# Low parts of the weights last in a block, partly on POOL, and a third output block at the last head of a matrix-memory layer

## The chip, the cores and the metric

The kernel runs on one core of a Trainium2 chip. The metric is the device time of one execution in microseconds (us): the median of three runs. One further execution was recorded by the hardware profiler. PE, ACT, DVE, POOL and SP are the tensor, scalar, vector, general (GpSimd) and sync engines; SP issues the loads of weights.

## The reference

A decoder trunk of two layers, each a token mixer and a gated MLP with a short convolution, with an RMSNorm before each. It has 320 tokens: one prompt of 256 and eight sequences of eight sampled tokens. The model width is 1024. Layer a mixes by spatial gating. Layer b, where the change lies, is a matrix memory (mLSTM) with 8 heads, keys of 128 and values of 256. Cut to what matters, for a head and its running state `C`, `n`, `m`:

```python
p = x @ w_in                       # q/k before the convolution, v, o, and the gates i and f
qk = silu(causal_dwconv(qk_pre, ...))
ig = i_pre + b_i;  lf = log_sigmoid(f_pre + b_f)
b = cumsum(lf);  D = b[t] - b[s] + ig[s]  (s <= t)
m_t = max(b + m, max_s D);  sc = (q @ k.T) * exp(D - m_t);  w = exp(b + m - m_t)
num = w * (q @ C) + sc @ v;  den = w * (q @ n) + sum(sc)
h = num / max(|den|, exp(-m_t))
C_new = decay * C + (k * g).T @ v
y = (sigmoid(o) * groupnorm(h)) @ w_out
```

The kernel takes all tokens of the prompt as one chunk. The outputs include the new states of the prompt and of the eight samples.

## The kernel before

**Products with weights.** A weight block is 1024 x 128 (8 k-tiles of 128 x 128), used against all 320 tokens. So that the product is nearly exact in a reduced input type, a block `raw` is split in two: the high part `wh`, a cast on ACT (L127), and the low part `wl` = raw - wh, a subtraction on DVE (L130). The tokens are split likewise into `xh` and `xl`. `chunk()` issues three matmuls per k-tile (wh with xh, wh with xl, wl with xh), 24 for a block of 8. `weights()` writes out the queue `wq` of all blocks in order; `prefetch()` loads up to four blocks ahead from SP (four buffers `raw`) and splits one block ahead (three buffers each of `wh` and `wl`); `take()` hands out the next one.

**What sets the order.** PE runs in the order in which the program issues its matmuls. On ACT, DVE, POOL and SP a scheduler orders the instructions; each engine then works through its own queue in order, and waits on semaphores of the others. Products of blocks go to three PSUM banks (`pm`), all else in layer b to five others.

**The gates.** `gates()` computes the rows of the input and forget gates for 8 heads, while PE multiplies the first six blocks of `b_win` (head 0: two of q/k, two of v, two of o). The rows pass through a multiply by the norm's row `rb`, a bias, a log-sigmoid in two tables on ACT (Exp, Ln), and two scans on DVE: the running sum `b` (L593) and the running maximum `M` (L598). From these come `X` (L609 and L610: M and the weights of the old state, split in high and low part), which the matmul `pMb` spreads over the partitions, and the rows `RS`, which are transposed to columns (`pt`, `cols`). In the trace most of these rows are called `g`.

**A head.** `scores(h)` makes the decay weights `w` from pMb (ACT), masks them with selects on POOL (L684 to L689) and multiplies the scores with them (`Pf`, split into `Ph`, `Pl`). `state_split` splits the old state `C` into `Ch` (ACT) and `Cl` (DVE, L758); `inter(h, i)` multiplies it with the queries `Qz`; `numer(h)` adds the products within the chunk to `num` and issues the statistics of the group norm, down to the power `sl` on POOL (L805). `k_nat` and `v_nat` transpose k and v (`pk`, `pv`), make `kgh`, `kgl`, `kgs` and, on POOL, `kgz` (L737); `v_nat` makes `vh`, `vl`. `state_prompt` (`pCp`) and `state_sample` (`pcs`) make the new states. `o_epi` makes the output gate (`o_b` on DVE, `th_o` on ACT). `finish(h)` transposes the normed head (`phn`) and makes its output halves `yhb` (ACT, L861) and `ylb` (DVE, L862). The loop over heads puts the work of head h-1 between the blocks of head h.

**The output product.** `b_wo` has eight output blocks over 16 k-tiles, two per head. Their first halves (k-tiles 0 to 7) are placed between heads 4 and 6 (`EARLY_OUT`). At the last head, `begin(0)` and `begin(1)` start the second halves of blocks 0 and 1 with the six k-tiles that are ready (8 to 13); the end of the layer closes them with the two of the last head and does the other six.

Of the kernel before, what the change touches and what calls it, by code (L numbers as in the profile page):

```python
# [19 lines left out]
NB, NS = 8, 8  # L20
# [17 lines left out]
class Net:  # L38
# [19 lines left out]
    def weights(self):  # L58

        I = self.I  # L60
        q = []

        def add(w, b, *groups, k0=0):
            for kn in groups:
                q.append((w, b, k0, kn))
                k0 += kn

        for b in range(4):
            add(I["a_wv"], b, 4, 4)
# [12 lines left out]

        ffn(0)
        add(I["b_wg"], 0, 8)
        for h in range(NH):
            for r in range(6):
                if (h, r) == (NH - 1, 4):
                    for b in (0, 1):
                        add(I["b_wo"], b, 6, k0=8)
# [3 lines left out]
        for b in range(KD):  # L93
            if b < 2:
                add(I["b_wo"], b, 2, k0=14)
            else:
                add(I["b_wo"], b, 8, k0=8)
        ffn(1)
        self.wq = q
        self.loaded, self.halved, self.used = [], [], 0  # L100

    AHEAD, SPLIT_AHEAD = 4, 1
    EARLY_OUT = {(4, 5): (0, 1), (5, 3): (2,), (5, 5): (3, 4), (6, 3): (5,), (6, 5): (6, 7)}

    def prefetch(self, n, m):

        nc = self.nc
        while len(self.loaded) < min(n, len(self.wq)):
            w, b, k0, kn = self.wq[len(self.loaded)]
            raw = self.wraw.tile([P, 8, P], F32, tag="raw", name="raw")  # L110
            nc.sync.dma_start(raw[:, :kn, :], w[b, :, k0:k0 + kn, :])
            self.loaded.append(raw)
        while len(self.halved) < min(m, len(self.wq)):
            i = len(self.halved)
            raw, kn = self.loaded[i], self.wq[i][3]
            self.loaded[i] = None
            wh = self.wsp.tile([P, 8, P], F32R, tag="wh", name="wh")
            wl = self.wsp.tile([P, 8, P], F32R, tag="wl", name="wl")
            if self.wq[i][0] is self.I["b_wg"]:

                nc.scalar.copy(wh[:, :, 64:], raw[:, :, 64:])
                nc.scalar.copy(wl[:, :, :64], raw[:, :, :64])
                nc.vector.tensor_tensor(wl[:, :, 64:], raw[:, :, 64:], wh[:, :, 64:].bitcast(F32), op=SUB)
                self.halved.append((None, wl))
                continue
            if i:
                self.last_split = nc.scalar.copy(wh[:, :kn, :], raw[:, :kn, :])  # L127
            else:
                nc.vector.tensor_copy(wh[:, :kn, :], raw[:, :kn, :])
            nc.vector.tensor_tensor(wl[:, :kn, :], raw[:, :kn, :], wh[:, :kn, :].bitcast(F32), op=SUB)  # L130
            self.halved.append((wh, wl))

    def take(self):
# [386 lines left out]
    def layer_b(self):  # L520
# [5 lines left out]
        with ExitStack() as ctx:  # L526
# [23 lines left out]
            def gates(rp):  # L550
                bif = rp.tile([8, 2 + NB], F32, name="bif")
                rst = rp.tile([8, 2, T], F32, name="rst")
                selr = rp.tile([40, NH, P], F32, name="selr")
# [9 lines left out]
                nc.gpsimd.memset(sel.bitcast(F32), 0.0)  # L563
                m0 = bif[:, 2:2 + NB]
# [27 lines left out]
                nc.vector.scalar_tensor_tensor(z, z, 0.0, az, op0=ALU.min, op1=SUB)  # L592
                nc.vector.tensor_tensor_scan(b, rst[:, 0, :], z, 0.0, op0=MULT, op1=ADD)  # L593
# [4 lines left out]
                nc.vector.tensor_tensor_scan(M, rst[:, 1, :], aM, -1e30, op0=ADD, op1=MAX)  # L598
                nc.vector.tensor_tensor(m, b, M, op=ADD)
# [4 lines left out]
                ML = M[:, TP + NS - 1::NS]  # L604
                nc.vector.tensor_copy(Xf[:, 0:T], M)
                nc.vector.tensor_tensor(seg(wi[:, :64]), m0.unsqueeze(2).to_broadcast([8, NB, NS]), seg(M[:, TP:]), op=SUB)
# [7 lines left out]

                nc.vector.tensor_copy(RS[0:8, 0:T], a)
                nc.vector.tensor_scalar(g[:, :TP], a[:, :TP], M[:, TP - 1:TP], None, op0=SUB)
# [157 lines left out]
            def numer(h):  # L774
                s = S[h]
                Ph, Pl, dec = s["P"]
                mv, dn = mvs[h % 2], dns[h % 2]
                num = [self.psa.tile([P, 512], F32, tag="pa", name="num") for _ in range(2)] + [s["num2"]]
# [6 lines left out]
                mm3(d, Ph[:, P:TP], Pl[:, P:TP], vh[:, 0, :], vl[:, 0, :], True, False)  # L785
                mm3(d, Ph[:, TP:384], Pl[:, TP:384], vh[:, 1, :], vl[:, 1, :], False, True)
                ns = hp.tile([64, CW], F32, tag="ns", name="ns", bufs=1)
                nc.scalar.copy(ns, num[2][64:, :CW])
# [106 lines left out]

            part = {}

            def begin(m):

                part[m] = self.psm.tile([P, 512], F32, tag="pm", name="pm")  # L900
                self.chunk(part[m], lambda k: Y[8 + k], True, False)

            for h in range(NH):
                if h:
# [9 lines left out]
                    early(h, 1)  # L914
                    v_epi(h, 0, blk())
                    state_prompt(h - 1)
# [22 lines left out]
                if h and not last:  # L939
                    state_sample(h - 1, 3)  # L940
                k_nat(h)
                v_nat(h)
                if h:
                    inter(h, 0)
                for i in (2, 3):
                    state_split(h, i)
                early(h, 5)
# [3 lines left out]
            begin(1)  # L951
            inter(h, 1)
            for i in (2, 3):
                inter(h, i)
            numer(h)
            o_epi(h, 0, blk())
            state_prompt(h)
            o_epi(h, 1, blk())
            finish(h)
            for i in range(4):  # L960
                state_sample(h, i)
            nc.sync.dma_start(O["nP"], nP)
            nc.sync.dma_start(O["nS"], nS)
            for m in range(KD):
# [3 lines left out]
                else:  # L968
                    self.chunk(ps, lambda k: Y[14 + k], False, True)
                self.residual_norm(m, ps, V_FFN + 8)  # L970


    def run(self):
        nc, tc, I, O = self.nc, self.tc, self.I, self.O
        with tc.tile_pool(name="const", bufs=1) as cp, tc.tile_pool(name="xp", bufs=1) as xp, \
# [21 lines left out]
            self.layer_a()  # L997
            self.ffn(0, V_MIX + 8)
            self.layer_b()
            self.ffn(1, None)  # L1000

# [13 lines left out]
def _lay_out(i):  # L1015
# [29 lines left out]
    for c in (0, 64):  # L1045
# [3 lines left out]
    a["b_wo"] = _blocks(i["b_w_out"][0])  # L1049
    a["b_if"] = np.ascontiguousarray(np.concatenate(  # L1050
        [i["b_bias_i"].T, i["b_bias_f"].T, i["state_mlstm_m"][0].T], axis=1))
    a["b_state"] = np.ascontiguousarray(i["state_mlstm_conv"][0].reshape(24, 16, P).transpose(2, 1, 0))
# [13 lines left out]
    a["bdt"] = ((q[:, None] // NS == q[None, :] // NS) & (q[:, None] <= q[None, :])).astype(f)  # L1066
    seg = np.zeros((8, 2, T), f)
    starts = [0] + list(range(TP, T, NS))
# [37 lines left out]
```

## Time and profile before

| | |
|---|---|
| median of three runs | 977.37 us (975.83 to 977.41) |
| profiled execution, its time | 975.58 us |
| its span | 973.9 us |
| its mean granted clock of PE | 0.996 |
| busy: PE, DVE, ACT, POOL | 961.7, 697.6, 514.5, 103.2 us |
| matmuls | 6513 |
| instructions | 17241 |
| layer b in the trace | about 425 to 731 us |

Engines work side by side, so their busy times do not add up. A line of a group names a source line, the engine, the operation, the output and inputs with shapes, a count, and after the bar the busy time, the mean of one in ns, and the idle time just before with what ended it. A line of the timeline begins with the start and the duration in us, and ends, where the engine waited, with the wait and what released it. Instructions of one kind that follow each other closely are one line there, with their count behind an x.

### The profile page before, as it was taken

To read this page: it belongs to the slowest core of one execution; us is meant where nothing else is said; L and a number is where in the kernel's file an instruction comes from. 1 tells how busy PE (TensorE), PEld (TensorE's weight loads), DVE (VectorE), ACT (ScalarE), POOL (GpSimd) and SP (SyncE) were. 2 spreads that over 40 slices of the span, in tenths; PEclk is the share of its full clock that TensorE was granted. 3 is DMA by queue.
4 is the path that set the end of the run, shared out by engine and by line. 5 is a ranking of instruction groups with operands and counts; after the bars stand their busy time and mean duration, and the time that the engine had idled before them with its cause. 6 is when DMAs were issued, how large, how long until landed. Compare 5 with 4: busy or idle time off the path is not lost.

```text
span 973.9 us, 17241 instructions
## 1 busy us (share of the span) xinstructions
PE 961.7 (99%) x6513; PEld 944.8 (97%) x6513; DVE 697.6 (72%) x1348; ACT 514.5 (53%) x922; POOL 103.2 (11%) x286
## 2 busy tenths in 40 slices
PE   9999999999999999999999999999999999999996
PEld 7889999999999999999999999999999999999996
DVE  6658975577777755469999978887787777775442
ACT  6557543454454443348766756565565455544432
POOL 3200000010000000013231111111101000000000
PEclk9999999999999999999999999999999999999998
DMA  8745444444444455555565565553464444445541
GB/s 264 234 136 165 128 129 151 151 148 152 150 144 147 146 153 152 154 176 174 175 205 168 185 200 167 170 189 120 140 204 138 152 150 152 151 147 149 152 125 54
DMA packets 56308, 154.60 MB, mean 159 GB/s; under 512 B 6642, under 2 KB 18290, under 8 KB 56226
## 3 DMA queue, kind: packets, MB, share of 16 engines
q1 hardware_dynamic: 56226, 153.51, 49.6%
q8 instruction: 51, 0.84, 0.4%
q14 instruction: 31, 0.25, 0.1%
HBM read 141.55 MB, written 11.94 MB: 158 GB/s over the span
## 4 chain that ended last, share of the span: by engine, by line
PE 82%; issue 10%; DVE 5%; ACT 2%; DMA 0%; POOL 0%; SPq 0%; DVEq 0%; POOLq 0%; ACTq 0%
PE pm L47 69%; PE pv_a L47 6%; PE num L47 2%; PE pcs L47 1%; PE pmix L47 1%; DVE wl L130 1%; DVE bcv L648 1%; DVE Cl L758 1%; PE pv L50 0%; ACT wh L127 0%; PE psc L47 0%; PE pCp L47 0%; PE phn L50 0%; DMA xT<-in_xT 0%; PE pg L47 0%
## 5 line engine op out<-in xcount | busy, mean ns | idle before, releaser
L127 ACT CAST wh<-raw 128x1024 fp32r<-128x1024 f32 (+2 forms) x253 | 257.0, 1016 | 341.4 <-PE pm L47 164.1
L130 DVE TENSOR_TENSOR wl<-raw,wh 128x1024 fp32r<-128x1024 f32 (+2 forms) x254 | 299.9, 1181 | 131.8 <-ACT wh L127 128.8
L47 PE MATMUL pm<-xh,wh 128*128 128x320 f32 x1216 | 378.1, 311 | 0.0
L47 PE MATMUL pm<-xh,wl 128*128 128x320 f32 x1216 | 376.0, 309 | 1.1 <-DVE wl L130 1.1
L47 PE MATMUL pm<-xl,wh 128*128 128x320 f32 x1216 | 375.6, 309 | 0.0
L47 PEld LDWEIGHTS pm<-xh,wl 128*128 128x128 f32 x1216 | 228.3, 188 | 1.6 <-DVE wl L130 1.6
L47 PEld LDWEIGHTS pm<-xh,wh 128*128 128x128 f32 x1216 | 228.4, 188 | 0.3
L47 PEld LDWEIGHTS pm<-xl,wh 128*128 128x128 f32 x1216 | 228.4, 188 | 0.3
L47 PE MATMUL pm<-yh_f,wh 128*128 128x320 f32 x352 | 109.0, 310 | 0.0
L47 PE MATMUL pm<-yh_f,wl 128*128 128x320 f32 x352 | 108.5, 308 | 0.0
L47 PE MATMUL pm<-yl_f,wh 128*128 128x320 f32 x352 | 108.5, 308 | 0.0
L47 PEld LDWEIGHTS pm<-yl_f,wh 128*128 128x128 f32 x352 | 66.1, 188 | 0.0
L47 PEld LDWEIGHTS pm<-yh_f,wh 128*128 128x128 f32 x352 | 66.1, 188 | 0.0
L47 PEld LDWEIGHTS pm<-yh_f,wl 128*128 128x128 f32 x352 | 66.1, 188 | 0.0
L442 DVE SCALAR_TENSOR_TENSOR fcv<-fpad,vecs,fcv 128x336 f32<-128x336 f32 x88 | 49.6, 565 | 2.2 <-ACT fcv L440 0.7
L239 DVE TENSOR_TENSOR xT<-pm,xT 128x320 f32<-128x320 f32 x40 | 19.5, 490 | 41.9 <-PE pm L47 41.9
L47 PE MATMUL pm<-ylb,wh 128*128 128x320 f32 x128 | 39.9, 312 | 0.5 <-DVE ylb L862 0.4
L47 PE MATMUL pm<-yhb,wh 128*128 128x320 f32 x128 | 40.0, 312 | 0.4 <-ACT yhb L861 0.4
L47 PE MATMUL pm<-yhb,wl 128*128 128x320 f32 x128 | 39.6, 309 | 0.0
L47 PE MATMUL pm<-yh_a,wh 128*128 128x320 f32 x128 | 39.6, 309 | 0.0
L47 PE MATMUL pm<-yh_a,wl 128*128 128x320 f32 x128 | 39.5, 308 | 0.0
L47 PE MATMUL pm<-yl_a,wh 128*128 128x320 f32 x128 | 39.5, 308 | 0.0
(269 smaller groups left out, 1386.5 us busy)
## 6 DMA issues: line engine op xcount, KB each, us to landing
raw<-in_f_up SPq DMA_DIRECT2D x88, 512.0 KB, 3.3
raw<-in_b_win SPq DMA_DIRECT2D x48, 512.0 KB, 3.7
raw<-in_f_dn SPq DMA_DIRECT2D x32, 448.0 KB, 3.3
C<-in_C SPq DMA_DIRECT2D x32, 258.0 KB, 3.4
raw<-in_a_win SPq DMA_DIRECT2D x16, 512.0 KB, 3.3
raw<-in_a_wo SPq DMA_DIRECT2D x16, 512.0 KB, 3.8
raw<-in_f_dn SPq DMA_DIRECT2D x16, 512.0 KB, 3.5
out_Cs<-C SPq DMA_DIRECT2D x32, 256.0 KB, 2.9
```

The costliest lines, as they stand in the source:

```text
L47: self.pin(self.nc.tensor.matmul(out, lhsT, rhs, start=start, stop=stop))
L127: self.last_split = nc.scalar.copy(wh[:, :kn, :], raw[:, :kn, :])
L130: nc.vector.tensor_tensor(wl[:, :kn, :], raw[:, :kn, :], wh[:, :kn, :].bitcast(F32), op=SUB)
L239: self.nc.vector.tensor_tensor(x, ps[:, :T], x, op=ADD)
L442: nc.vector.scalar_tensor_tensor(cv, pd[:, i:i + NC], self.vec(w + i * KF), cv, op0=MULT, op1=ADD)
L648: nc.vector.scalar_tensor_tensor(cv, pd[:, i:i + NC], self.vec(w + 16 * i), cv, op0=MULT, op1=ADD)
L758: nc.vector.tensor_tensor(Cl, C0, Ch.bitcast(F32), op=SUB)
```

## The change

It has five parts.

1. In layer b alone (`low_last`), `chunk()` issues the 16 products of a block that use `wh` first, then the 8 that use `wl`.
2. For 18 of the 48 blocks of `b_win` (blocks 2 to 5, and the two v blocks of heads 1 to 7, among them 8 and 9) the low part is computed on POOL instead of DVE.
3. The two gates lie in one tile of 40 partitions (input gate in 0 to 7, forget gate in 32 to 39), so that one multiply and one add serve both; two rows are written in place, so two copies go. The bias and the scan's constants are laid out to match by the host.
4. `numer()` is cut in two: the statistics (`stats`) are issued behind the next block of PE, and the scheduler has to place them behind the last split of weights on ACT and on the engine of the last low part.
5. The order at the first and last heads: at head 0 two `state_split` come before `k_nat`; at the last head `begin(0)` takes four k-tiles instead of six, `inter(7, 0)` and one `state_split` come behind `begin(1)`, and a third block, `begin(2)`, is issued behind the last `pcs`. The queue of weights follows.

```diff
+    POOL_LOW = (2, 3, 4, 5) + tuple(6 * h + r for h in range(1, NH) for r in (2, 3))
+    low_last = False
...
-            nc.vector.tensor_tensor(wl[:, :kn, :], raw[:, :kn, :], wh[:, :kn, :].bitcast(F32), op=SUB)
+            w, b, _, _ = self.wq[i]
+            eng = nc.gpsimd if w is self.I["b_win"] and b in self.POOL_LOW else nc.vector
+            self.last_low = eng.tensor_tensor(wl[:, :kn, :], raw[:, :kn, :], wh[:, :kn, :].bitcast(F32), op=SUB)
...
+    def behind_split(self):
+        with self.tc.issue_after(self.last_split.ins), self.tc.issue_after(self.last_low.ins):
+            yield
...
     def chunk(self, ps, rhs, first, last):
         (wh, wl), kn = self.take()
-        for k in range(kn):
-            xh, xl = rhs(k)
-            self.mm(ps[:, :T], wh[:, k, :], xh, first and k == 0, False)
-            self.mm(ps[:, :T], wh[:, k, :], xl, False, False)
-            self.mm(ps[:, :T], wl[:, k, :], xh, False, last and k == kn - 1)
+        for sweep in ((0, 1) if self.low_last else (2,)):
+            for k in range(kn):
+                xh, xl = rhs(k)
+                if sweep != 1:
+                    self.mm(ps[:, :T], wh[:, k, :], xh, first and k == 0, False)
+                    self.mm(ps[:, :T], wh[:, k, :], xl, False, False)
+                if sweep:
+                    self.mm(ps[:, :T], wl[:, k, :], xh, False, last and k == kn - 1)
...
-                ig, z, az, b, a, M, m, aM, g = [row("g" + str(i)) for i in range(9)]
+                b, m, aM, g = [row("g" + str(i)) for i in range(4)]
+                zi, az = [rp.tile([40, T], F32, name=n) for n in ("zi", "az")]
+                ig, z, az = zi[:8], zi[32:], az[32:]
+                a, M = RS[0:8, 0:T], Xf[:, 0:T]
...
-                nc.vector.tensor_tensor(z, gr[32:40], self.rb[32:40, :], op=MULT)
-                nc.vector.tensor_tensor(ig, gr[0:8], self.rb[0:8, :], op=MULT)
+                nc.vector.tensor_tensor(zi, gr[:40], self.rb[:40, :], op=MULT)
                 qk_epi(0, 0, p0)
-                nc.vector.tensor_scalar(z, z, bif[:, 1:2], None, op0=ADD)
-                nc.vector.tensor_scalar(ig, ig, bif[:, 0:1], None, op0=ADD)
+                nc.vector.tensor_scalar(zi, zi, bif[:, 0:1], None, op0=ADD)
...
-                nc.vector.tensor_copy(Xf[:, 0:T], M)
...
-                nc.vector.tensor_copy(RS[0:8, 0:T], a)
...
-                    v_epi(h, 0, blk())
+                    ps = blk()
+                    with self.behind_split():
+                        stats(h - 1)
+                    v_epi(h, 0, ps)
...
             begin(1)
-            inter(h, 1)
-            for i in (2, 3):
+            inter(h, 0)
+            state_split(h, 3)
+            for i in (1, 2, 3):
                 inter(h, i)
             numer(h)
-            o_epi(h, 0, blk())
+            ps = blk()
+            stats(h)
+            o_epi(h, 0, ps)
             state_prompt(h)
             o_epi(h, 1, blk())
             finish(h)
             for i in range(4):
                 state_sample(h, i)
+            begin(2)
...
-                    self.chunk(ps, lambda k: Y[14 + k], False, True)
+                    self.chunk(ps, lambda k: Y[done[m] + k], False, True)
```

More of the change, by code (lines that the diff above doesn't have):

```diff
@@ L1 @@
-from contextlib import ExitStack
+from contextlib import ExitStack, contextmanager
 import numpy as np
@@ L87, in weights @@
                 if (h, r) == (NH - 1, 4):
-                    for b in (0, 1):
-                        add(I["b_wo"], b, 6, k0=8)
+                    add(I["b_wo"], 0, 4, k0=8)
+                    add(I["b_wo"], 1, 6, k0=8)
                 add(I["b_win"], 6 * h + r, 8)
@@ L92, in weights @@
                     add(I["b_wo"], b, 8)
[L93 to L97, printed above, removed]
+        add(I["b_wo"], 2, 6, k0=8)
+        add(I["b_wo"], 0, 4, k0=12)
+        for b in (1, 2):
+            add(I["b_wo"], b, 2, k0=14)
+        for b in range(3, KD):
+            add(I["b_wo"], b, 8, k0=8)
         ffn(1)
@@ L550, in gates @@
             def gates(rp):
-                bif = rp.tile([8, 2 + NB], F32, name="bif")
-                rst = rp.tile([8, 2, T], F32, name="rst")
+                bif = rp.tile([40, 1 + NB], F32, name="bif")
+                rst = rp.tile([40, 2, T], F32, name="rst")
                 selr = rp.tile([40, NH, P], F32, name="selr")
@@ L563, in gates @@
                 nc.gpsimd.memset(sel.bitcast(F32), 0.0)
-                m0 = bif[:, 2:2 + NB]
+                m0 = bif[:8, 1:1 + NB]
                 def row(name, n=T):
                     return rp.tile([8, n], F32, name=name)
-                ig, z, az, b, a, M, m, aM, g = [row("g" + str(i)) for i in range(9)]
+                b, m, aM, g = [row("g" + str(i)) for i in range(4)]
+                zi, az = [rp.tile([40, T], F32, name=n) for n in ("zi", "az")]
+                ig, z, az = zi[:8], zi[32:], az[32:]
                 Xf = row("Xf", 392)
+                a, M = RS[0:8, 0:T], Xf[:, 0:T]
                 wi = row("wi", 72)
@@ L592, in gates @@
                 nc.vector.scalar_tensor_tensor(z, z, 0.0, az, op0=ALU.min, op1=SUB)
-                nc.vector.tensor_tensor_scan(b, rst[:, 0, :], z, 0.0, op0=MULT, op1=ADD)
+                nc.vector.tensor_tensor_scan(b, rst[32:, 0, :], z, 0.0, op0=MULT, op1=ADD)
                 nc.vector.tensor_tensor(a, ig, b, op=SUB)
@@ L597, in gates @@
                 nc.vector.tensor_tensor(aM[:, TP::NS], a[:, TP::NS], m0, op=MAX)
-                nc.vector.tensor_tensor_scan(M, rst[:, 1, :], aM, -1e30, op0=ADD, op1=MAX)
+                nc.vector.tensor_tensor_scan(M, rst[:8, 1, :], aM, -1e30, op0=ADD, op1=MAX)
                 nc.vector.tensor_tensor(m, b, M, op=ADD)
@@ L786, in numer, with stats @@
                 mm3(d, Ph[:, TP:384], Pl[:, TP:384], vh[:, 1, :], vl[:, 1, :], False, True)
+                s["num"] = num
+            def stats(h):
+                s = S[h]
+                num, mv, dn = s.pop("num"), mvs[h % 2], dns[h % 2]
                 ns = hp.tile([64, CW], F32, tag="ns", name="ns", bufs=1)
@@ L894, in blk @@
                 return self.block(KD, self.x_rhs)
-            part = {}
+            part, done = {}, {}
             def begin(m):
                 part[m] = self.psm.tile([P, 512], F32, tag="pm", name="pm")
+                n = self.wq[self.used][3]
                 self.chunk(part[m], lambda k: Y[8 + k], True, False)
+                done[m] = 8 + n
             for h in range(NH):
@@ L940, in layer_b @@
                     state_sample(h - 1, 3)
+                if not h:
+                    for i in (2, 3):
+                        state_split(h, i)
                 k_nat(h)
@@ L943, in layer_b @@
                 if h:
-                    inter(h, 0)
-                for i in (2, 3):
-                    state_split(h, i)
+                    if not last:
+                        inter(h, 0)
+                    for i in (2,) if last else (2, 3):
+                        state_split(h, i)
                 early(h, 5)
@@ L951, in layer_b @@
             begin(1)
-            inter(h, 1)
-            for i in (2, 3):
+            inter(h, 0)
+            state_split(h, 3)
+            for i in (1, 2, 3):
                 inter(h, i)
             numer(h)
-            o_epi(h, 0, blk())
+            ps = blk()
+            stats(h)
+            o_epi(h, 0, ps)
             state_prompt(h)
@@ L998, in run @@
             self.ffn(0, V_MIX + 8)
+            self.low_last = True
             self.layer_b()
+            self.low_last = False
             self.ffn(1, None)
@@ L1049, in _lay_out @@
     a["b_wo"] = _blocks(i["b_w_out"][0])
-    a["b_if"] = np.ascontiguousarray(np.concatenate(
-        [i["b_bias_i"].T, i["b_bias_f"].T, i["state_mlstm_m"][0].T], axis=1))
+    a["b_if"] = np.zeros((40, 1 + NB), w.dtype)
+    a["b_if"][:8] = np.concatenate([i["b_bias_i"].T, i["state_mlstm_m"][0].T], axis=1)
+    a["b_if"][32:, 0] = i["b_bias_f"][0]
     a["b_state"] = np.ascontiguousarray(i["state_mlstm_conv"][0].reshape(24, 16, P).transpose(2, 1, 0))
@@ L1066, in _lay_out @@
     a["bdt"] = ((q[:, None] // NS == q[None, :] // NS) & (q[:, None] <= q[None, :])).astype(f)
-    seg = np.zeros((8, 2, T), f)
+    seg = np.zeros((40, 2, T), f)
     starts = [0] + list(range(TP, T, NS))
```

2 lines of the change are left out of this document (1 added, 1 removed).

## The prediction

> **What bounds the kernel now.** I read the page first (engine shares, costliest groups), then the windows of layer b, the waits of PE, and the timeline around each wait.
>
> ```profile
> span 973.9 us, 17241 instructions
> PE 961.7 (99%) x6513; PEld 944.8 (97%) x6513; DVE 697.6 (72%) x1348; ACT 514.5 (53%) x922; POOL 103.2 (11%) x286
> L130 DVE TENSOR_TENSOR wl<-raw,wh 128x1024 fp32r<-128x1024 f32 (+2 forms) x254 | 299.9, 1181 | 131.8 <-ACT wh L127 128.8
> ```
> ```profile
> 436.00:470.00 34.00, 32.75 (x231) 31.89 (x229) 32.59 (x82) 30.05 (x62) 11.64 (x30) 1.00 0.46 155
> 540.00:665.00 125.00, 125.00 (x901) 124.98 (x900) 102.58 (x239) 73.99 (x161) 19.06 (x36) 1.00 0.55 176
> ```
> ```profile
> PE pm L47 <- DVE wl L130: 1.1, 2, 0.7
> PE pm L47 <- ACT yhb L861: 0.4, 1, 0.4
> PE pm L47 <- DVE ylb L862: 0.4, 2, 0.2
> PE num L47 <- DVE Cl L758: 0.3, 2, 0.2
> ```
>
> The columns of the windows are the stretch, its length, and the busy time of PE, weight load, DVE, ACT and POOL. PE works in 961.7 of 973.9 us, and the change leaves the number of matmuls as it is. In the middle of layer b (540 to 665 us) PE is busy in all 125 us, so nothing that relieves DVE there can shorten anything. Only two places of layer b have time to give: the stage of the gates and head 0 (436 to 470 us: PE 32.75 of 34, while DVE has 32.59 and is the busiest engine but for PE), and the last head. The waits name the four things that PE is short of: low parts of weights, the last head's output halves and the low parts of the matrix memory. Their size comes from the starts of the matmuls:
>
> ```profile
> 453.38 0.31 PE L47 MATMUL pm<-xl,wh 128*128 128x320 f32 x1
> 456.60 0.31 PE L47 MATMUL pm<-xh,wl 128*128 128x320 f32 x1
> 446.90 0.31 PE L47 MATMUL pm<-xl,wh 128*128 128x320 f32 x1
> 447.88 0.31 PE L47 MATMUL pm<-xh,wh 128*128 128x320 f32 x1
> 469.05 0.30 PE L47 MATMUL pm<-xl,wh 128*128 128x320 f32 x1
> 470.29 0.31 PE L47 MATMUL pm<-xh,wh 128*128 128x320 f32 x1
> 703.88 0.31 PE L47 MATMUL pm<-yhb,wh 128*128 128x320 f32 x1
> 706.14 0.31 PE L47 MATMUL pm<-yhb,wl 128*128 128x320 f32 x1
> ```
>
> From the first pair, 22 matmuls start in 3.22 us, 0.147 us each. From 446.90 to 447.88 two starts take 0.98 us instead of 0.29 (0.69 lost, a wait for wl); from 469.05 to 470.29 two take 1.24 (0.95 lost, wl again); from 703.88 to 706.14 five take 2.26 instead of 0.73 (1.53 lost, on the last head's halves). The two waits for Cl and the other one for ylb are 0.5 us together by the view and, with the restart that made 0.64 of the last head's waits into 1.53, some 1.2. So about 4.4 us is all that the change can win. A measurement of this kernel can tell about 0.2%, 1.95 us, from no change.
>
> **Low parts last.** In a block of 8 k-tiles the 16 products with wh now come first, so wl is wanted 16 x 0.147 = 2.35 us after the block's start instead of 0.29, and the wh buffer comes free 8 x 0.147 = 1.17 us earlier. Both known waits for wl are under 1 us, so this alone removes them: 0.69 at the gates, 0.95 behind head 0. In the heads between, PE has no wait and it is worth 0.
>
> **Eighteen low parts on POOL.** A wl costs DVE 1.18 us. POOL's price is not in the trace for this operation; the nearest rows are these, and they also show what the two engines do to each other:
>
> ```profile
> L737 POOL TENSOR_TENSOR kgz<-kgs,mk 128x1024 fp32r<-128x1024 f32 x8 | 15.2, 1898 | 65.5 <-DVE kgs L736 65.5
> L296 POOL TENSOR_TENSOR ws_a<-ws_a,trit 128x1024 f32<-128x1024 f32 x1 | 2.4, 2411 | 0.0
> ```
> ```profile
> 456.47 1.29 DVE L758 TENSOR_TENSOR Cl<-C,Ch 128x516 fp32r<-128x516 f32 x2
> 458.23 1.90 POOL L737 TENSOR_TENSOR kgz<-kgs,mk 128x1024 fp32r<-128x1024 f32 x1 [3.20 <-DVE kgs L736]
> 459.23 2.06 DVE L758 TENSOR_TENSOR Cl<-C,Ch 128x516 fp32r<-128x516 f32 x2
> 678.04 0.85 POOL L805 TENSOR_TENSOR sl<-t,mhalf 128x3 f32<-128x3 f32 x1 [6.51 <-DVE t L803]
> 501.54 1.76 POOL L805 TENSOR_TENSOR sl<-t,mhalf 128x3 f32<-128x3 f32 x1 [3.14 <-DVE t L803]
> 501.37 1.22 DVE L130 TENSOR_TENSOR wl<-raw,wh 128x1024 fp32r<-128x1024 f32 x1
> ```
>
> I take 1.90 us (eight cases, the same size and output type) and keep 2.41 as the other end. The pair of Cl takes 1.29 us alone, but 2.06 where it meets kgz: kgz ends at 460.13, and 460.13 + 1.29 = 461.42 is nearly the pair's end at 461.29. So DVE stood until POOL was through. The other way round, sl takes 0.85 us alone and 1.76 where a wl of DVE runs from 501.37 to 502.59. I read this as exclusion: an instruction of DVE that reads two operands from SBUF and a tensor operation of POOL do not run beside each other, and whoever is in holds it to its end. An instruction of DVE that reads PSUM leaves POOL room to get in. Then moving a wl does not take 1.18 from DVE: it puts 1.90 in its place wherever DVE's neighbours read SBUF.
>
> [...]
>
> Six of the eighteen (blocks 2 to 5, 8 and 9) lie at the gates and head 0, the other twelve in heads 2 to 7, two each. There DVE is busy in 102.58 of 125 us, 18% of it is free, and a head has at least six blocks of 24 x 0.147 = 3.5 us, so 3.8 us of DVE free; exclusion costs at most 2 x (1.90 - 1.18) = 1.4. I take 0; if that cover were gone, up to 1.4 each. Head 0 has no such cover.
>
> **Gates in one tile.** One multiply and one add of DVE go, and two copies:
>
> ```profile
> 445.42 0.31 DVE L615 COPY RS<-g 8x320 f32<-8x320 f32 x1
> 445.65 0.81 DVE L598 TENSOR_TENSOR_SCAN g<-rst,g 8x320 f32<-8x320 f32 x1
> 446.39 1.19 DVE L130 TENSOR_TENSOR wl<-raw,wh 128x1024 fp32r<-128x1024 f32 x1
> 448.38 0.31 DVE L605 COPY Xf<-g 8x320 f32<-8x320 f32 x1
> 450.22 0.56 DVE L610 TENSOR_TENSOR X<-Xf,X 8x392 fp32r<-8x392 f32 x1
> 450.92 1.22 DVE L130 TENSOR_TENSOR wl<-raw,wh 128x1024 fp32r<-128x1024 f32 x1
> 451.21 0.42 PE L47 MATMUL pMb<-X,sel 128*128 128x392 f32 x1
> ```
>
> The chain to watch ends in X, which pMb needs: X is done at 450.78, PE arrives at 451.21. The first saved multiply and add lie ahead of the logarithm, which ACT's table loads hold, so they bring 0. Behind it the copies go (2 x 0.31) and so does the wl of block 5 (1.19, now on POOL). But in the new order of DVE the wl of block 6 stands ahead of the second scan and that of block 7 ahead of the first copy to X (before, they stood behind X, at 450.92 and after): + 2 x 1.2. Sum 2.4 - 0.62 - 1.19 = +0.6. Block 5's POOL instruction falls among scans, subtractions and bcv, which read SBUF: by exclusion + 1.9, and 0.1 for block 4's. X comes at 450.78 + 2.6 = 453.4, and pMb 2.2 us later than before; without exclusion X comes at 451.4, pMb 0.2 later. (The wait of 0.69 that goes is inside these figures.)
>
> **Head 0 behind it.** POOL's queue is in order, and the new one has the wl of block 8 ahead of the memsets and of head 0's selects:
>
> ```profile
> 449.71 0.47 DVE L845 TENSOR_TENSOR o_b<-pm,rb 128x320 f32<-128x320 f32 x1
> 450.22 0.47 ACT L847 ACTIVATE th_o<-o_b 128x320 f32<-128x320 f32 x1
> 451.06 1.05 ACT L127 CAST wh<-raw 128x1024 fp32r<-128x1024 f32 x1 [0.37 <-PE pm L47]
> 451.57 0.21 POOL L879 MEMSET Ps<- 128x128 f32 x1 [2.83 <-issue]
> 453.90 0.54 POOL L684 TENSOR_SCALAR_AFFINE_SELECT w<-w 128x128 f32<-128x128 f32 x2
> 454.75 0.28 POOL L689 TENSOR_SCALAR_AFFINE_SELECT w<-w 64x64 f32<-64x64 f32 x1
> 457.20 0.39 PE L47 MATMUL num<-Cl,Qz 128*128 128x258 f32 x1 [0.17 <-DVE Cl L758]
> ```
>
> Memsets take 451.57 to 453.90, selects 1.13 more. The wl of block 8 waits for its wh, and that cast stands behind th_o on ACT, which waits for o_b on DVE, queued behind the gate chain. With that chain 2.6 later: o_b at 452.3, th_o 452.8 to 453.3, wh to 454.3, wl to 456.2, memsets to 458.5, selects to 459.6. Then the new DVE order has a short Pf, a vl (0.7 us together) and the first Cl (0.65); Pf and vl read PSUM, so kgz gets in right there and holds Cl for 1.9. Cl ends at 459.6 + 1.9 + 0.65 = 462.15; before, the first of the pair at 456.47 ended at 457.12. So the first num is 5.0 us later, the delay of pMb included. What waits behind: every later matmul, since PE is in program order. Without exclusion, wh is done at 450.7 to 452.1, wl 1.9 later, selects end at 456.0 to 457.4, Cl at 457.4 to 458.8: 0.3 to 1.7 later, mean 1.0.
>
> **The last head.** begin(2), 18 matmuls, and 4 of block 0 now stand between the last pcs and the first product that needs yhb and ylb: 22 x 0.147 = 3.2 us.
>
> ```profile
> 705.29 0.55 DVE L862 SCALAR_TENSOR_TENSOR ylb<-y_b,gnh,yhb 128x320 fp32r<-128x320 f32 x1
> ```
>
> The halves were ready at 705.84, and even with one more wl (1.2) ahead of them that is 707.0, against a need at 703.88 + 3.2 = 707.1. The 1.53 goes. The third PSUM bank is held longer, but bank 0 is closed 2 blocks before it is wanted again: 0. The reordered inter and pv save 0 to 0.5 at the earlier wait for ylb, since the Cl behind it is late next. 1.5 to 2.0, I take 1.8. Splitting numer moves DVE work behind a split and, with no PE wait there, costs 0 (at most one wl, 1.2, if DVE were late).
>
> **Sum**, against the profiled execution (span 973.9, time 975.58, so 1.7 around the span; it lies 1.79 under the median 977.37): +5.0 - 0.95 - 1.8 = +2.25, a profiled time of 977.8, and on the median 979.6.
>
> **Rivals.**
> - A, *no exclusion where it counts*: POOL slips in beside instructions of DVE that read PSUM. For it: some of DVE's work there (o_b, cols, vl, bpad) reads PSUM. Against: the pair of Cl. +1.0 - 0.95 - 1.8 = -1.75: 975.6, from -2.7 to -0.8 by the ends.
> - B, *head 0 costs nothing*, the one that ends faster: wh buffers free 1.17 us earlier put block 8's cast ahead of th_o's wait, and its wl on POOL is over when the selects' operand arrives. Then only the gains stay, -2.75, with 2.0 for the last head -2.95: 974.6 and 974.4. It decides in head 0: whether the first num's Cl ends before 457.12 + 2.75 = 459.9; later than that the change loses. The order on ACT (cast behind th_o) speaks against it.
> - C, *POOL's subtraction takes 2.41*: block 4's holds bcv and the logarithm 1.0 longer, blocks 5 and 8 0.5 each: 2.0, of which 0.5 meets slack: 981.1.
>
> [...]
>
> **How the numbers follow.** Forecast 0.42 (975.58 + 2.25 is just over the bound: slower 0.36, same 0.06), A 0.27 (same 0.18, faster 0.09), B 0.23 (faster 0.22, same 0.01), C 0.08 (slower). Faster 0.31, same 0.25, slower 0.44. The range goes from B's far end (974.4) less 0.8, half of the 1.58 between the runs shown, to C's 981.1 plus 1.4 if block 9's POOL instruction delays head 0 as well: 973.6 to 982.5. The forecast's own range is 978.5 to 981.
>
> **What would show it.** Right: a Cl or scan of DVE stretched beside a wl of POOL; wl on POOL near 1.9; pMb waiting near 453.4 and head 0's selects near 458.5; no wait on wl in layer b; no gap behind the last pcs. Wrong: selects before 456, pMb without a wait, or gaps in heads 1 to 6, where I expect none.

## The result

| | before | after |
|---|---|---|
| median | 977.41 us (975.83 to 977.9, 5 runs) | 986.47 us (985.57 to 987.16, 5 runs) |
| ratio | | 1.0095 (1.008 to 1.0109) |
| profiled execution, its span | 973.9 us | 984.6 us |

The change is 9.1 us slower. I had forecast slower, by 2.2: the direction holds, and the size is outside the range (982.5 at most).

First, where the time lies. The span is 10.7 us longer. These are the first memset of the gates, an addition to the residual late in head 6, and the last one of layer b, each in the timeline of before and then of after:

```profile
425.43 0.42 POOL L561 MEMSET RS<- 128x384 f32 x1
661.89 0.49 DVE L239 TENSOR_TENSOR xT<-pm,xT 128x320 f32<-128x320 f32 x1 [1.32 <-PE pm L47]
728.49 0.49 DVE L239 TENSOR_TENSOR xT<-pm,xT 128x320 f32<-128x320 f32 x1 [0.50 <-PE pm L47]
```
```profile
426.74 0.42 POOL L578 MEMSET RS<- 128x384 f32 x1
671.42 0.49 DVE L255 TENSOR_TENSOR xT<-pm,xT 128x320 f32<-128x320 f32 x1 [1.90 <-PE pm L47]
739.28 0.49 DVE L255 TENSOR_TENSOR xT<-pm,xT 128x320 f32<-128x320 f32 x1 [1.03 <-PE pm L47]
```

Layer b begins 1.31 us later, although nothing ahead of it was changed; among the profiled runs below, this memset lies anywhere from 424.99 to 427.31. So 1.3 of the 10.7 is scatter of layer a and has to be taken off before stages are compared. The gates and the heads to head 6 then lose 9.53 - 1.31 = 8.2 us, the last head 10.79 - 9.53 = 1.3.

The longest waits of PE in layer b in the trace of after, and four windows (the first with PE, weight load, DVE, ACT and POOL as before; the others of PE alone, with its granted clock behind the bracket):

```profile
PE pt L50 <- ACT RS L634: 3.6, 1, 3.6
PE num L47 <- DVE Cl L774: 3.2, 3, 2.2
```
```profile
436.00:470.00 34.00, 27.85 (x169) 26.43 (x168) 29.82 (x57) 23.26 (x45) 18.63 (x29) 0.90 0.48 155
480.00:660.00 180.00, 180.00 (x1305) 1.00 0.55 181
...
457.00:458.00 1.00, 1.00 (x5) 0.50 0.89 348
...
467.00:468.00 1.00, 1.00 (x5) 0.50 0.24 93
```

No wait for wl is left, as forecast. In its place PE stands 3.6 us ahead of pt (the transposed gate rows), then 1.0 and 0.5 at the first num, and 2.2 in the last head. From 480 to 660 us it is busy throughout, with 1305 matmuls as before: the low parts on POOL there cost nothing. And one thing was in no step of the prediction: between 436 and 470 us the granted clock of PE is 0.90 on the mean, because it falls to 0.50 twice; a matmul then starts every 0.27 instead of 0.147 us.

What POOL and DVE do to each other, in the group of the low parts on POOL and in the timeline of after:

```profile
L136 POOL TENSOR_TENSOR wl<-raw,wh 128x1024 fp32r<-128x1024 f32 x18 | 44.6, 2480 | 49.0 <-ACT wh L131 35.7
```
```profile
438.77 2.51 POOL L136 TENSOR_TENSOR wl<-raw,wh 128x1024 fp32r<-128x1024 f32 x1 [1.43 <-ACT wh L131]
439.26 2.40 DVE L664 SCALAR_TENSOR_TENSOR bcv<-bpad,vecs,bcv 128x344 f32<-128x344 f32 x1
441.69 0.49 ACT L666 ACTIVATE bth<-bcv 128x344 f32<-128x344 f32 x1 [1.22 <-DVE bcv L664]
446.42 3.12 POOL L136 TENSOR_TENSOR wl<-raw,wh 128x1024 fp32r<-128x1024 f32 x1 [4.28 <-ACT wh L131]
447.20 2.52 DVE L613 COPY g<-RS 8x320 f32<-8x320 f32 x1
450.27 1.21 DVE L136 TENSOR_TENSOR wl<-raw,wh 128x1024 fp32r<-128x1024 f32 x1
451.41 0.81 DVE L616 TENSOR_TENSOR_SCAN Xf<-rst,g 8x320 f32<-8x320 f32 x1
456.16 0.56 DVE L627 TENSOR_TENSOR X<-Xf,X 8x392 fp32r<-8x392 f32 x1
456.77 0.69 PE L47 MATMUL pMb<-X,sel 128*128 128x392 f32 x1 [0.18 <-DVE X L627]
456.81 2.37 POOL L136 TENSOR_TENSOR wl<-raw,wh 128x1024 fp32r<-128x1024 f32 x1 [3.30 <-ACT wh L131]
461.45 0.54 POOL L700 TENSOR_SCALAR_AFFINE_SELECT w<-w 128x128 f32<-128x128 f32 x2
462.50 2.03 DVE L713 TENSOR_TENSOR Qz<-qw,Qz 128x64 fp32r<-128x64 f32 x1
462.56 1.89 POOL L753 TENSOR_TENSOR kgz<-kgs,mk 128x1024 fp32r<-128x1024 f32 x1
464.84 0.36 PE L47 MATMUL num<-Ch,Qz 128*128 128x258 f32 x1 [1.01 <-DMA C<-in_C]
465.71 0.39 PE L47 MATMUL num<-Cl,Qz 128*128 128x258 f32 x1 [0.51 <-DVE Cl L774]
```

This is the forecast's chain, later at each step. Beside block 4 (at 438.77) bcv takes 2.40 us (0.58 elsewhere), and ACT stands 1.22 us for it, ahead of the table load of the logarithm (1.28 us, at 442.20). Beside block 5 (446.42) a plain copy of 8x320, a form that took 0.31 before, takes 2.52, until POOL ends at 449.54. Block 6's wl goes ahead of the second scan. X is done at 456.72, block 8's wl (456.81) holds back the selects, and kgz comes in beside the small Qz (0.21 before, 2.03 here). For the first num the view names a load of C; but the C that it needs had been cast at 461.41, while Qz, which it reads too, was ready only at 464.53.

### The profile page after: what moved, and what is told of

It reads as the page before. It is cut to its first block, busy times and chain, and to the rows that moved or that the text cites. A ratio compares the mean times of both kernels' runs of the same rounds, so it can differ in the third digit from the quotient of the medians.

```text
span 984.6 us, 17266 instructions
## 1 busy us (share of the span) xinstructions
PE 965.8 (98%) x6513; PEld 949.2 (96%) x6513; DVE 697.8 (71%) x1327; ACT 517.7 (53%) x923; POOL 148.8 (15%) x304
## 4 chain that ended last, share of the span: by engine, by line
PE 83%; issue 10%; DVE 4%; ACT 1%; DMA 1%; POOL 0%; DVEq 0%; SPq 0%; POOLq 0%; ACTq 0%
PE pm L47 69%; PE pv_a L47 6%; PE num L47 2%; PE pcs L47 1%; PE pmix L47 1%; DMA raw<-in_b_win 1%; PE psc L47 1%; DVE wl L136 1%; PE pCp L47 1%; PE pv L50 0%; PE phn L50 0%; DVE bcv L664 0%; DVE Cl L774 0%; DMA xT<-in_xT 0%; PE pk L50 0%
## 5 line engine op out<-in xcount | busy, mean ns | idle before, releaser
L131 ACT CAST wh<-raw 128x1024 fp32r<-128x1024 f32 (+3 forms) x254 | 257.1, 1013 | 316.4 <-PE pm L47 158.4
L47 PE MATMUL pm<-xh,wh 128*128 128x320 f32 x1216 | 373.5, 312 | 0.0
L47 PE MATMUL pm<-xl,wh 128*128 128x320 f32 x1216 | 371.0, 309 | 0.0
L136 DVE TENSOR_TENSOR wl<-raw,wh 128x1024 fp32r<-128x1024 f32 (+3 forms) x237 | 279.1, 1178 | 123.6 <-ACT wh L131 120.9
L47 PE MATMUL pm<-xh,wl 128*128 128x320 f32 x1216 | 321.3, 309 | 0.0
L47 PEld LDWEIGHTS pm<-xh,wl 128*128 128x128 f32 x1216 | 214.4, 188 | 0.0
L136 POOL TENSOR_TENSOR wl<-raw,wh 128x1024 fp32r<-128x1024 f32 x18 | 44.6, 2480 | 49.0 <-ACT wh L131 35.7
L47 PE MATMUL pm<-ylb,wh 128*128 128x320 f32 x128 | 37.8, 309 | 0.0
```

Of the source, the lines that this page charges most:

```text
L47: self.pin(self.nc.tensor.matmul(out, lhsT, rhs, start=start, stop=stop))
L136: self.last_low = eng.tensor_tensor(wl[:, :kn, :], raw[:, :kn, :], wh[:, :kn, :].bitcast(F32), op=SUB)
```

## The experiments

Each is one kernel; "against" is the kernel before on the same chip in the same hour, whose median was 976.8 to 977.2.

**No low part on POOL**, all else as in after:

```diff
-    POOL_LOW = (2, 3, 4, 5) + tuple(6 * h + r for h in range(1, NH) for r in (2, 3))
+    POOL_LOW = ()
```

> The changed kernel with every low part on DVE (POOL_LOW empty), all else kept. Theory POOL: its subtractions (2.4 to 3.1 us each in the trace of after, with DVE standing beside them) cost the 8 us that the gates and head 0 lost, so this run falls to about 978 to 979, with no PE wait over 1 us at pt and PE's clock back at 1.00 there; the last head's wait for Cl stays. Theory order: the new queue of DVE (a low part ahead of the second scan, one tile for the gates) costs them whichever engine subtracts: 983 or more.

979.80 us against 977.20, ratio 1.0029 (1.0018 to 1.004): some 6.5 us of the 9.1 were the subtractions on POOL. The waits at pt are down to 0.2 us. But 2.6 stay, more than the last head's share, and the clock is not back at 1.00 as I had expected: it falls to 0.50 once at head 0, behind 0.8 and 1.1 us of waiting at the first num; see below.

**Blocks 2 to 5 back on DVE**, and **only the twelve of heads 2 to 7 on POOL**:

```diff
+    POOL_LOW = tuple(6 * h + r for h in range(1, NH) for r in (2, 3))     # first kernel
+    POOL_LOW = tuple(6 * h + r for h in range(2, NH) for r in (2, 3))     # second kernel
```

> The changed kernel with blocks 2 to 5 back on DVE; blocks 8 and 9 and the twelve of heads 2 to 7 stay on POOL. Theory POOL, by place: the four at the gates cost most (6 us of the 8), blocks 8 and 9 some 2, the twelve later ones nothing: 980 to 981. If the memsets and selects behind block 8 on POOL's queue are the main thing: 983 to 985. Theory order: 985 or more, no different from the changed kernel.

> The changed kernel with only the twelve low parts of heads 2 to 7 on POOL. By my prediction these cost 0, since PE has no wait there: as with none on POOL, 979.8, within 0.7. If they cost by their number, two thirds of the 6.7 between none and eighteen: 984. The last head's own (wl stretched beside kgz) is in both.

983.86 (ratio 1.0064, 1.0051 to 1.0076) and 979.06 (1.0022, 1.0012 to 1.0032). Counted against the kernel before of their own hour, the three lose 2.6 (none on POOL), 2.2 (the twelve) and 6.7 us (the twelve with blocks 8 and 9). So the twelve cost nothing, blocks 8 and 9 some 4.5 us, and blocks 2 to 5 the other 2.4, each with an uncertainty of 1.6 to 1.9 by the intervals, and in this order of taking them away. The subtractions cost by their place, not by their number. I had expected the four at the gates to cost most; blocks 8 and 9 cost no less, and the memsets and selects of head 0 stand behind block 8 on POOL. In the trace with blocks 8 and 9 on POOL, PE stands once at head 0, for 4.2 us. The view names a load of C; but the first of these was issued at 452.9, and no load of C took more than 7.0 us to land, so it was there before 460. The timeline shows what came last: the cast of C on ACT, queued behind those of the masked scores:

```profile
452.02 2.67 POOL L136 TENSOR_TENSOR wl<-raw,wh 128x1024 fp32r<-128x1024 f32 x1 [2.70 <-ACT wh L131]
456.96 0.54 POOL L700 TENSOR_SCALAR_AFFINE_SELECT w<-w 128x128 f32<-128x128 f32 x2
460.21 0.25 ACT L263 CAST Ps<-Pf 64x64 fp32r<-64x64 f32 x1 [1.56 <-DVE Pf L718]
460.73 0.61 ACT L773 CAST Ch<-C 128x516 fp32r<-128x516 f32 x1
461.44 0.35 PE L47 MATMUL num<-Ch,Qz 128*128 128x258 f32 x1 [4.22 <-DMA C<-in_C]
```

**The kernel before with the 18 on POOL alone:**

```diff
+            eng = nc.gpsimd if w is self.I["b_win"] and b in self.POOL_LOW else nc.vector
+            eng.tensor_tensor(wl[:, :kn, :], raw[:, :kn, :], wh[:, :kn, :].bitcast(F32), op=SUB)
```

> The kernel before with only the 18 low parts moved to POOL; order of products, gates and last head as before. Theory POOL: at least the 8 us, and more, since wl is wanted 2 us sooner without the new order of products: 985 to 992, with PE waits on wl from POOL. Theory order: 977 to 979.

990.03, ratio 1.0132 (1.0119 to 1.0146), 3.8 us more than the whole change loses, and with a wait of 2.3 us for wl from POOL that the trace of after does not have. So the new order of products seems to hide some of POOL's slowness.

**The last head's order as before**, all else as in after:

```diff
-            inter(h, 0)
-            state_split(h, 3)
-            for i in (1, 2, 3):
+            inter(h, 1)
+            for i in (2, 3):
...
-            begin(2)
```

> The changed kernel with the last head's order and its queue of weights as before (begin(0) with six k-tiles, inter(7,0) ahead of begin(1), no begin(2)). In the trace of after, that head lost 2.4 us at a wait for Cl behind a DVE subtraction stretched to 2.24 us beside kgz, and 1.5 net over the head. Theory last head: that wait goes and the old gap behind the last pcs (1.5) comes back: 985 to 986 against 986.5. If the wait for Cl stays with the old order, 988; if low parts last alone removes the old gap, 984.

985.65 against 986.47, ratio to before 1.0093 (1.0078 to 1.0109): the wait of 2.2 goes, those for yhb and ylb come back, a difference of some 0.8 that these few runs do not separate. In after's last head, the timeline shows the cause:

```profile
698.43 1.90 POOL L753 TENSOR_TENSOR kgz<-kgs,mk 128x1024 fp32r<-128x1024 f32 x1 [4.18 <-DVE kgs L752]
699.17 2.24 DVE L136 TENSOR_TENSOR wl<-raw,wh 128x1024 fp32r<-128x1024 f32 x1
702.38 0.69 DVE L774 TENSOR_TENSOR Cl<-C,Ch 128x516 fp32r<-128x516 f32 x1
703.12 0.39 PE L47 MATMUL num<-Cl,Qz 128*128 128x258 f32 x1 [2.20 <-DVE Cl L774]
```

Cl stands behind a wl that kgz holds until 700.33. That the moved split put it there is my reading: this run takes back the split, the order of inter and begin(2) together.

**The parts alone, on the kernel before**: low parts last, the gates' tile, and a third output block.

```diff
+            self.low_last = True                     # first kernel
             self.layer_b()
...
+                nc.vector.tensor_tensor(zi, gr[:40], self.rb[:40, :], op=MULT)     # second, with the rest of gates()
...
             for i in range(4):
                 state_sample(h, i)
+            begin(2)                                 # third, with its six k-tiles in the queue
```

> The kernel before with only the new order of products in layer b (wh products of a block first, wl products last). By my prediction the two waits for wl (0.69 and 0.95 us) go: 975.8 against about 977.3. Rival: the wait moves to what stands next in line (the gate rows, Cl, kgz at head 0) and the time stays at 977.3, or is 1 to 2 us later since DVE's queue comes in another order: 978 to 979.

> The kernel before with only the two gates in one tile (one multiply, one add and two copies less on DVE). Theory: PE does not wait on the gates before, so nothing: 977.3, within 0.5. Rival: the scheduler places DVE's low parts otherwise around the shorter chain and a wait arises: 978 to 980.

> The kernel before with only a third output block begun (six k-tiles, 18 matmuls) behind the last pcs; begin(0), begin(1), inter and the splits stay where they were. Theory: the gap of 1.53 us behind the last pcs is covered and nothing else moves: 975.8. Rival: the gap is taken over by a wait on the third block's weights or on its PSUM bank: 977.3.

979.57 (1.0026, 1.0017 to 1.0036), 976.21 (0.999, 0.9981 to 0.9999) and 977.15 (1.0003, 0.9994 to 1.0011). Low parts last does remove the waits for wl, but it costs 2.5 us; the gates' tile gains some 0.9 (0.1 to 1.9 by the interval); the third block gains nothing, since a wait of 1.2 us for wl follows it: a closing product of two k-tiles is over before the next block is split. With the last head's 1.3, the parts add up to 2.5 - 0.9 + 1.3 = 2.9, near the 2.6 that stay without POOL, though parts need not add up. The split of `numer()` was not run by itself.

**Is it kgz?** In the run with low parts last alone, PE waits for Cl, and Cl stands beside kgz. The same two kernels, the low parts last alone and after without POOL, with head 0's kgz on DVE:

```diff
-                nc.gpsimd.tensor_tensor(kgz, ...
+                (nc.gpsimd if h else nc.vector).tensor_tensor(kgz, ...
```

> Low parts last alone (as in b_low, 979.57), with head 0's kgz made by DVE instead of POOL; it comes right behind the first pair of Cl in DVE's queue. In b_low that pair took 3.00 us beside kgz on POOL (2.34), against 1.29 alone, and PE waited 1.55 and 0.74 us for it. Theory exclusion: the pair is back at 1.3 and the wait of 1.55 goes, though DVE now pays some 1.2 for kgz: 977.5 to 978.3. Theory queue (DVE's order at the gates, two low parts ahead of cols, is late by itself): 979 to 980.

> The changed kernel without any low part on POOL (979.8), with head 0's kgz on DVE. Beside kgz, Pl took 1.96 us there (0.54 alone), and PE stood 0.8 and 1.1 us at the first num, with a window of half clock behind. Theory exclusion: Pl is back at 0.54, kgz takes 1.2 on DVE ahead of Cl, PE stands under 1 us in all and the half clock goes: 977.5 to 978.5, what is left being the last head's. Theory queue: DVE's sum stays the same and so does the time, 979.5 to 980.

977.69 (ratio 1.0009, 1.0 to 1.0018; was 979.57) and 978.46 (1.0019, 1.0009 to 1.0029; was 979.80). The timeline of low parts last with kgz on POOL, then with kgz on DVE:

```profile
459.42 3.00 DVE L762 TENSOR_TENSOR Cl<-C,Ch 128x516 fp32r<-128x516 f32 x2
459.53 2.34 POOL L741 TENSOR_TENSOR kgz<-kgs,mk 128x1024 fp32r<-128x1024 f32 x1 [2.31 <-ACT Ch L761]
462.48 0.39 PE L47 MATMUL num<-Cl,Qz 128*128 128x258 f32 x1 [1.55 <-DVE Cl L762]
```
```profile
458.78 1.51 DVE L762 TENSOR_TENSOR Cl<-C,Ch 128x516 fp32r<-128x516 f32 x2
460.20 1.22 DVE L741 TENSOR_TENSOR kgz<-kgs,mk 128x1024 fp32r<-128x1024 f32 x1
```

DVE takes on 1.2 us more work and the kernel is 1.9 us faster (1.5 with each counted against the kernel before of its own hour): the wait of 1.55 is gone, and the pair of Cl is back from 3.00 to 1.51. The exclusion is shown by taking POOL's instruction away. The other run gains 0.9 to 1.3 in the same two ways of counting, which the intervals do not separate from nothing; the half clock that I expected to go remains in it.

**A stand of PE by itself.** The kernel before, with the gate rows held by a chain of multiplies by 1.0:

```diff
+                for _ in range(14):        # the second kernel: 4
+                    nc.vector.tensor_scalar(Xf, Xf, 1.0, None, op0=MULT)
                 nc.vector.tensor_copy(X[0:8], Xf)
```

> The kernel before with 14 multiplies by 1.0 of the gate rows (Xf, 8x392, some 0.34 us each, one after another, 4.8 us in all) ahead of the first copy to X. The rows reach PE 4.8 us later, PE arrives 0.4 us after they were ready, so PE stands about 4.4 us ahead of pMb. Theory clock: behind a stand of that length PE's granted clock falls to about 0.57 for some 3 to 4 us, as it did behind the stand of 3.6 us in the changed kernel, and the run loses 1.5 to 2.5 us more than the stand: 983 to 984.5. Theory no clock effect of the stand (the fall had another cause): PE's rows show 1.00 and the run loses what the stand takes: 981.5 to 982.

> The kernel before with 4 multiplies by 1.0 of the gate rows in a chain. Fourteen held PE for 8.55 us, 0.64 each, so four hold it for some 2.1 us. In the runs so far the granted clock fell to 0.50 for one window of 3.41 us where PE had stood at least 1.55 us of the window before, and did not where 2.2 us fell half into each of two windows. Theory windows: the stand of 2.1 costs either 2.1 alone (979.5) or 2.1 + 1.7 (981), by where it falls, and the runs of this kernel lie in both places. Theory length (a fall only behind a single stand above some 3 us): always 979.5 and no row at 0.50 in layer b.

985.36 (1.0086, 1.0067 to 1.0104) and 982.99 (1.0067, 1.0049 to 1.0086). The stands were longer than I had sized them, 8.5 and 3.8 us, since the scheduler put other work of DVE between the links, three wl among it in the long chain. Where the links follow each other, eight take 3.05 us:

```profile
454.43 0.34 DVE L610 TENSOR_SCALAR Xf<-Xf 8x392 f32<-8x392 f32 x1
454.70 1.21 DVE L130 TENSOR_TENSOR wl<-raw,wh 128x1024 fp32r<-128x1024 f32 x1
455.84 3.05 DVE L610 TENSOR_SCALAR Xf<-Xf 8x392 f32<-8x392 f32 x8
```

So the second was no test of a stand of 2 us, and the times alone do not separate my theories: the long one loses 8.3 us by the medians, no more than its stand. The traces do, with the start of layer b taken off (425.44 and 427.11, against 425.43 before). In them pMb comes 8.8 and 4.0 us later than before, and the end of layer b 9.9 and 5.5. So another 1.1 and 1.5 us are lost behind the stand, although the wait for wl behind head 0 has gone.

The granted clock, in windows of 1 us behind the long stand, and in windows around two short stands of another run, after without POOL and with kgz on DVE:

```profile
455.00:456.00 1.00, 0.00 (x0) 0.71 0.49 102
...
464.00:465.00 1.00, 1.00 (x5) 0.50 1.06 332
465.00:466.00 1.00, 1.00 (x7) 0.67 0.90 293
```
```profile
455.50:459.00 3.50, 2.12 (x14) 0.99 1.02 323
459.00:462.00 3.00, 3.00 (x13) 0.50 0.97 369
...
691.00:694.40 3.40, 1.46 (x11) 1.00 0.13 39
694.50:697.80 3.30, 3.30 (x16) 0.50 0.47 156
```

Behind the long stand the clock is at half for 10.2 us, 5.7 of it after PE is back at 460.0. In the other run PE misses 1.4 and 1.9 of some 3.4 us and has half clock in the 3.4 us that follow; these two falls begin at 458.95 and 694.45 us. In after the two falls begin at 456.30 and 466.55, 10.25 apart, and last 3.41 and 3.40 us. The 10.25 are three such stretches, and the 235.5 between the other two are 69 of them, 3.413 each. Carried on from 456.30 by 71 and 72 steps of 3.413, the bounds of a stretch lie at 698.6 and 702.0. The last head of after has a stand of 2.2 us with no fall behind it, and by these bounds 1.1 of it falls into each of two stretches:

```profile
698.60:702.00 3.40, 2.32 (x18) 1.00 0.32 108
702.00:705.40 3.40, 2.28 (x18) 1.00 0.20 63
705.50:708.80 3.30, 3.30 (x26) 1.00 0.36 130
```

My reading of these traces is a decision in fixed stretches of 3.4 us: PE that missed enough of one (1.4 and 1.9 us above) runs at a clock of 0.50 in the next, which by my estimate costs up to 1.7 us, half of 3.41, if it is busy then. No single long gap was needed: stands of 0.57 and 0.81 us, together 1.4 in one stretch, came ahead of a fall. How much is enough is not settled. After without POOL, which has the same last head, missed 1.8 of the stretch that begins 68 such steps behind its fall at head 0 (458.86 us), and kept its clock:

```profile
690.97:694.38 3.41, 1.61 (x13) 1.00 0.13 38
694.39:697.79 3.40, 3.26 (x24) 1.00 0.36 99
```

So between 1.4 and 1.8 both happen, and the missed time alone does not decide.

**A version that beats both.** The kernel before with low parts last only from head 1 on, so that the queues at the gates and head 0 stay, and the third block behind the last pcs; with and without the gates' tile:

```diff
             for h in range(NH):
+                self.low_last = h > 0
...
+            begin(2)
```

> The kernel before with three parts of the change, placed by the runs so far: one tile for the gates, the new order of products only from head 1 on (so that the queues at the gates and head 0 stay as in the kernel with the gates' tile alone), and a third output block begun behind the last pcs; no low part on POOL. Theory: the gains add up, 0.6 to 0.9 (gates, wait for wl there) + 0.95 (wl behind head 0) + 1.5 (gap behind the last pcs, its successor wait for wl covered by the order of products): 974 against 977.1. Rival: the waits move on as they did with low parts last everywhere: 976 to 978.

> The same without the gates' tile: the new order of products from head 1 on, and the third output block. If the parts add up, 0.6 to 0.9 over the run before it: 974.7. If the order of products from head 1 on disturbs head 0's rows, 977 or more in both.

With the tile 975.30 (0.9987, 0.9978 to 0.9996), without it 974.75 (0.9978, 0.9969 to 0.9987): 2.1 us faster than before. These are the wait for wl of the one without the tile and its windows at the gates and at the last head (PE before: 32.75 of 34 and 39.92 of 41):

```profile
PE pm L47 <- DVE wl L132: 0.4, 1, 0.4
```
```profile
436.00:470.00 34.00, 33.35 (x237) 32.73 (x236) 32.53 (x82) 30.28 (x64) 11.26 (x28) 1.00 0.45 153
665.00:706.00 41.00, 40.42 (x297) 39.75 (x296) 33.85 (x96) 23.18 (x60) 6.95 (x11) 1.00 0.37 119
```

The wait at 469 and the gap behind the last pcs are gone. The tile's 0.9 did not add up here (I had expected the one with it to be the faster); why is open.

## Why the prediction was right or wrong

- *Bound, and where there is time to give*: right. Heads 1 to 6 stayed full, and the twelve low parts there cost 0.
- *Exclusion of POOL and DVE*: right as a mechanism, and shown by kgz (the pair of Cl took 3.00 us beside it on POOL, 1.51 with it on DVE). It reaches further than I put it: the plain copy of 8x320 stood beside POOL as well (2.52 for 0.31), so it takes no two operands. That DVE leaves POOL room where it reads PSUM stood in the prediction without a figure; the traces have it: before, kgz took its 1.90 beside a pair of vl of 0.87 (458.18), and in after a wl on POOL took 2.37 (467.62) beside a pair of 0.86.
- *POOL's price, 1.90 us*: **wrong**. It measured 2.48 on the mean, 3.12 at most. I chose the row with the same output type (kgz, 1.90) over the nearest operation (ws_a, 2.41); kgz itself stayed at 1.89, so its form was a poor model. Rival C, at 0.08, had the 2.41; its total of 981.1 was still 5.4 short, since the price was not the main miss.
- *pMb 2.2 us later*: it came at 456.77, 5.56 after the 451.21 of before, 4.25 with the start of layer b taken off. I counted 0.1 for block 4 and 1.9 for block 5; bcv lost 1.8 and the copy 2.2. The term that failed is block 4's: bcv's delay passed to the logarithm over ACT's queue, and I had counted almost nothing for it.
- *The first num 5.0 later*: **mis-sized**. The one that waits for Cl came at 465.71, 7.2 later net (457.20 before). The chain (cast behind th_o, wl, memsets, selects, kgz into the gap) was right in order; every link had the later gates ahead of it, and it was Qz, ahead of Cl, that kgz held.
- *No term for the clock*: **missing**. Two stretches ran at half speed. The first (456.30 to 459.71) cost little: PE still stood 1.0 and 0.5 us at the first num, for a chain that ran on POOL and DVE. The second (466.55 to 469.95) cost up to 1.7. The sum said 5.0 - 0.95 = 4.1 for gates and head 0, and 8.2 was measured; 2.2 of the difference is in the first num, and the second stretch makes most of the other 1.9, with a further wait of 0.46 for Cl.
- *-0.95 behind head 0, and low parts last "alone removes them"*: half right. The waits for wl went, but alone the part costs 2.5: DVE's queue came in another order, with two wl ahead of the columns, and Cl ran into kgz. I had costed a new order of PE's work without what it does to the queues of others.
- *The last head, -1.8*: **wrong sign**, +1.3, and with 3.1 us the largest single error of the sum. The gap behind the last pcs did go. I took the moved split and inter for free; Cl then stood behind a wl that kgz stretched to 2.24: a wait of 2.2.
- *The gates' tile, 0 ahead of the logarithm*: about right, some 0.9 faster alone.

In the traces, layer b lost 9.5 us (10.79 less the 1.31 of its start) where the sum had 2.25. Of the 7.2 between them, the first num has 2.2, the rest of head 0 1.9 and the last head 3.1.

## What to carry to other kernels

Here an instruction moved from VectorE to GpSimd was not moved off VectorE: instructions of VectorE beside it that read SBUF alone stood (2.52 us instead of 0.31 for a copy, 2.40 instead of 0.58 for bcv). Where a trace shows this, price such a move as a hold of both engines for the slower one's time (2.48 us on the mean here), and look at which instructions and which waits those are. Move such work only where the trace shows no wait of the bounding engine. Waits of TensorE that added up to 1.4 us and more within 3.4 us had, in some places of these traces, a second price, a clock of 0.50 for the 3.4 us behind them, which a sum of waits does not show; and where a scheduler sets the queues, a change in the order of one engine's work has to be read on the others too.

## What the runs showed of the hardware

POOL's subtraction of 128x1024 took 2.37 us where DVE left it room, and up to 3.12 beside DVE. A copy that reads SBUF alone waited for block 5's (2.52 instead of 0.31), while o_b and cols, which read PSUM, took 0.49 and 0.45 beside block 8's, as before (0.48 and 0.44). PE's granted clock fell to 0.50 for stretches of 3.4 us (in after from 456.30 to 459.71 and from 466.55 to 469.95). In layer b of these traces it fell behind full-speed stretches in which PE missed from 1.4 to 3.4 us, and never behind one in which it missed 1.3 or less; between 1.4 and 1.8 it fell behind some and not behind others, and what decides there is open. From this I estimate that a stand of 2 us costs between 2 and 3.7 (half of a stretch, 1.7, more) by where it falls. I think that this is why runs of after without POOL lie from 977.07 to 981.42; neither was tried by itself. The shift of layer a between executions (the first memset of the gates lies from 424.99 to 427.31 us) is not explained.
